# Layer 1's projections of a two-layer backbone: the recurrence's input first, its pieces paced wider

## The chip, the core and the metric

The kernel runs on one core of one Trainium2 chip. The metric is the device time of one execution in microseconds (us); the median of several runs counts.

## The reference, cut to what matters

Two layers work on 1024 latent tokens and 256 context tokens of width 1024. The change lies at the start of layer 1's token mixer:

```python
def mixer_cd(hl, hc, w_in, ...):
    xb_l, gt_l, cq_l, ckv_l, kr_l = split(hl @ w_in)
    xb_c, gt_c, cq_c, ckv_c, kr_c = split(hc @ w_in)
    hf_l, hf_c = rglru_direction(xb_l, xb_c, ..., False)
    hb_l, hb_c = rglru_direction(xb_l, xb_c, ..., True)
    c_l = ((hf_l + hb_l) * jax.nn.gelu(gt_l.astype(jnp.float32))).astype(hl.dtype)
    qn_l, qr_l = mla_q(cq_l, q_norm, w_uq)
    kn_l, v_l = mla_kv(ckv_l, kv_norm, w_ukv)
    kn_c, v_c = mla_kv(ckv_c, kv_norm, w_ukv)
    d_l = mla_latent(qn_l, apply_rope(qr_l, cos, sin), qr_l, kn_l, apply_rope(kr_l, cos, sin), v_l,
                     kn_c, kr_c, v_c)
```

The input, already normed and modulated, is projected to five parts: the recurrence's input xb (512 columns), its gate gt (512), the queries cq (384), keys and values ckv (256) and the rotary key kr (32). The recurrence (a gated linear recurrence, forward and backward, that starts in the context) needs xb of latent and context tokens. cq and ckv are each divided by the root of their mean square per token before the attention uses them.

## The kernel before, in words

Everything is kept transposed: features on the 128 partitions, tokens along the free axis, in three groups of tokens g = 0, 1 (512 latent tokens each) and 2 (256 context tokens). A float32 product is made of three fp32r matmuls per 128 rows of the contraction (`gemm`, L310 on: high weight by high and low input, low weight by high input, L315 to L317), so one projection of one weight tile of 128 columns by one group is 8 x 3 = 24 matmuls into one PSUM bank. There are four such banks (`bank`). A weight tile is loaded by a DMA on SP's queue (`load_w`, L290) into one of two buffers, split on ScalarE (L295) and on GpSimd or VectorE by turns (L298) into one of two pairs of buffers.

`proj1` (L1095 on) makes layer 1's projections by a string of letters, `PROJ1`: x (`p_xb`, four weight tiles for groups 0 and 1, then the same four for group 2), c (`p_cq`, three tiles, groups 0 and 1), k (`p_kv`, two tiles, three groups), g (`p_gt`, four tiles, groups 0 and 1) and r (`p_kr`, one tile, three groups). Results of x, c and k are copied out of PSUM by VectorE (L1157, L1110) and stored to HBM; those of g go through Gelu on ScalarE (L1203); those of r are rotated by VectorE (L1184 to L1188).

Beside the projections run flows: generators that yield a number of units and go on when that many have been pumped. Each projection pumps 8 x max(256, tokens) / 800 units into every flow:

```python
        pump(n * max(256, ps.shape[1]) / 800.0)
```

A projection of 512 tokens is worth 5.12 units, one of 256 tokens 2.56. `drain` runs a flow to its end at once. The instructions of each engine come into an order that a planner makes from this order of writing, and it lets an instruction that is ready go ahead of one that isn't. The flows here:

- "norm": the end of layer 0 for the context (`update`, `postnorm`, `prenorm`, L480 on). It waits YU = 14 units for a reload of x, 3 for the first root, 4 x 1.5 in the post-norm, 18 x 0.6 ahead of the second root, 6 for it and 4 x 2 in the pre-norm, whose tiles hh and hl (L496 to L503) are the input of group 2. Who asks for group 2 earlier forces the flow on (`Lazy`).
- "lru": the recurrence (`lru`, L995 on), in four blocks of 128 features. A block: load xb, 3 units; taps of the convolution on VectorE (L1013, L1017), eight instructions; wait `LY[0]` (10 for block 0); four gates of three matmuls (L1035, two passes each) and three sigmoids (L1036), `LY[1]` after each; tanh; the next block's taps, if its input is there; `LY[2]`; exponentials and squares on ScalarE, two products on VectorE (L1051); `LY[3]`; square roots (L1054); `LY[4]`; for each of two directions a product (L1057) and two scans (L1059, L1061) on VectorE, `LY[5]` after each; a sum on GpSimd (L1063) and the store to hsd (L1064). Block i may start when the context part of x's tile i is written. The gates' buffers r and i are two each: a block's gates need the scans of the block before to be done.
- "nrm": the norms of c and k (`normed`, `fin`, L1100 on). After `KY[0]` units, for each group: sums over partitions by small matmuls (L436), a chain of eleven small VectorE instructions for the inverse root (L440 to L445) and the diagonal tile dg (L452); `YR` = 6 units later a matmul that spreads the root (L457), a reload, the scaling (L1123) and a store; then `KY[1]` units. The squares are summed in a tile with the tag "sq", of which there are three, and dg is one of them too; therefore `normed` drains "nrm" before it begins.
- "mul": the recurrence's output times the gate (L1138 to L1142), from 30 units after both are there.

Ahead of g's last tile (`VW` = 3) the attention's value weights are loaded and split into two pages of a pool of 24. After the last projection "lru" and "nrm" are drained. Then the attention (`mla`) opens its pool where the recurrence's tiles lay: its first tile, va, is filled by ten memsets on GpSimd (L1258), which wait until the memory is free; keys and values are reloaded (L1220) and split (L321, L322), and TensorE starts with the values (L1274 to L1276) and keys.

Of the kernel before, what the change touches and what calls it, by code (L numbers as in the profile page):

```python
# [34 lines left out]
SQB = 3  # L35
# [19 lines left out]
PVD = 4  # L55
PB1 = 6
VW = 3
KY = 3.0, 8.0
CW0 = 2
YU = 14.0  # L60
PACE = 2.3
N0 = "SG"
QE0 = "VGG"
LY = (2.0, 1.0, 1.0, 2.0, 1.0, 1.0)
GY = 30.0, 4.0
DH = "s"
DL = "s"
QE00 = "GVV"
KE = "VV"
LY0 = 10.0  # L70
PROJ1 = "cxkgr"
ORD0 = "BABABABABB"

PO1 = (), ("n+++++nn",)
# [24 lines left out]
def tile_backbone(ctx: ExitStack, tc: tile.TileContext, a: dict, out: bass.AP):  # L99
# [23 lines left out]
    def nm(s):  # L123
        uid[0] += 1
        return f"{s}{uid[0]}"
# [78 lines left out]
    def tmp(n=512, dt=F32):  # L204
        return tp.tile([128, 512], dt, tag="t512", name=nm("t"), bufs=4)[:, 0:n]
# [254 lines left out]
    class Sq:  # L460

        def __init__(self, n, plan="n+++++++", eng="G"):
            self.n, self.acc, self.plan, self.eng, self.i = n, [], plan, V if eng == "V" else G, 0

        def add(self, src):
            new = self.i == 0 or self.plan[self.i] == "n"
            self.i += 1
            t = tp.tile([128, 512], F32, tag="sq", name=nm("sq"), bufs=SQB)[:, 0:self.n] if self.i == 1 else tmp(self.n)
            S.activation(t, src, AF.Square)  # L469
            if new:  # L470
                self.acc.append(t)
            else:
                self.eng.tensor_add(self.acc[-1], t, self.acc[-1])  # L473

    def rstd(sq, d, res, yr=YR):
        dg = rstd_a(sq.acc, sq.n, d)
        yield yr
        res.append(rstd_b(dg, sq.n))
# [616 lines left out]
    def proj1(hs, w, pa, tab, KR, wv):  # L1095

        def x5(s, n):
            return pa.tile([128, 1289], F32, tag=s, name=nm(s), bufs=n)

        def normed(nt, gs, c0, dst, key, d):  # L1100
            drain("nrm")
            sq = [Sq(TOK[g]) for g in gs]
            for i in range(nt):
                wt = wcol(w, c0 + i * 128)
                for g in gs:
                    n = TOK[g]
                    ps = bank()[:, 0:n]
                    gemm(ps, wt, *hs[g])
                    t = tmp(n)
                    V.tensor_copy(t, ps)  # L1110
                    nc.sync.dma_start(dst[:, i, OFF[g]:OFF[g] + n], t)
                    sq[g].add(t)

            def fin():
                yield KY[0]
                for g in gs:
                    n = TOK[g]
                    r = []
                    yield from rstd(sq[g], d, r)
                    for i in range(nt):  # L1120
                        t = tmp(n)
                        nc.sync.dma_start(t, dst[:, i, OFF[g]:OFF[g] + n])
                        V.scalar_tensor_tensor(t, t, cols(key, i), r[0], ALU.mult, ALU.mult)  # L1123
                        nc.sync.dma_start(dst[:, i, OFF[g]:OFF[g] + n], t)
                    yield KY[1]
            spawn(fin(), "nrm")

        def gated(i, key):
            ready.setdefault(i, set()).add(key)
            if len(ready[i]) < 2:  # L1130
                return

            def mul():
                yield GY[0]
                for g in range(2):
                    sl = slice(OFF[g], OFF[g] + 512)
                    t, t2 = tmp(), tmp()
                    nc.sync.dma_start(t, cld[:, i, sl])  # L1138
                    nc.sync.dma_start(t2, hsd[:, i, sl])
                    yield GY[1]  # L1140
                    V.tensor_mul(t, t, t2)
                    nc.sync.dma_start(cld[:, i, sl], t)  # L1142
            spawn(mul(), "mul")

        ready, todo = {}, set()
        GW, sp, tiny = lru_setup(pa)
        spawn(lru(todo, x5, GW, sp, tiny, gated), "lru")
        def p_xb():
            for gs in ((0, 1), (2,)):
                for i in range(4):  # L1150
                    wt = wcol(w, i * 128)
                    for g in gs:
                        n = TOK[g]
                        ps = bank()[:, 0:n]
                        gemm(ps, wt, *hs[g])
                        t = tmp(n)
                        V.tensor_copy(t, ps)  # L1157
                        nc.sync.dma_start(xbd[:, i, OFF[g]:OFF[g] + n], t)
                    if gs == (2,):
                        todo.add(i)  # L1160

        def p_cq():
            normed(3, (0, 1), 1024, cqd, "qn", 384)

        def p_kv():
            normed(2, (0, 1, 2), 1408, kvd, "kvn", 256)

        def p_kr():

            wkr = load_w(w[:, 1664:1696].rearrange("(k p) m -> p k m", p=128), 8, 32)  # L1170
            stg = wrp.tile([128, 8, 128], F32, tag="wr", name=nm("stg"))
            G.memset(stg[:, :, 0:64], 0.0)
            gcopy(stg[:, :, 96:128], wkr[:, :, 0:32])
            rot_w(stg[:, :, 64:96], wkr[:, :, 0:32])
            wt = split_w(stg)
            for g in range(3):
                n = TOK[g]
                ps = bank()[:, 0:n]
                gemm(ps, wt, *hs[g])
                sl = slice(OFF[g], OFF[g] + n)  # L1180
                if g < 2:
                    t = tmp(n)
                    t2 = tmp(n)
                    V.tensor_mul(t[64:96], ps[64:96], tab[64:96, sl])  # L1184
                    V.tensor_mul(t2[64:96], ps[96:128], tab[96:128, sl])
                    V.tensor_add(KR[64:96, sl], t[64:96], t2[64:96])
                else:
                    V.tensor_copy(KR[96:128, sl], ps[96:128])  # L1188

        def p_gt():  # L1190
            for i in range(4):
                if i == VW:
                    raw = wrp.tile([128, 8, 128], F32, tag="wr", name=nm("wr"))
                    src = a["mla_w_ukv"][0].rearrange("(k p) (h t m) -> t p k h m", p=128, t=2, m=64)
                    for k in range(2):
                        nc.sync.dma_start(raw[:, 4 * k:4 * k + 4].rearrange("p a (h m) -> p (a h) m", m=64), src[1, :, k])
                    wv.extend(split_w(raw, pages=True))
                wt = wcol(w, 512 + i * 128)
                for g in range(2):
                    ps = bank()  # L1200
                    gemm(ps, wt, *hs[g])
                    t = tmp()
                    S.activation(t, ps, AF.Gelu_apprx_tanh)  # L1203
                    DQ[DL].dma_start(cld[:, i, OFF[g]:OFF[g] + 512], t)
                gated(i, "g")

        for p in PROJ1:
            {"x": p_xb, "c": p_cq, "k": p_kv, "r": p_kr, "g": p_gt}[p]()
        drain("lru")
        drain("nrm")  # L1210
# [616 lines left out]
```

## Time and profile before

| what | us |
|---|---|
| median of three runs | 3098.53 |
| lowest, highest run | 3087.58, 3100.79 |
| the profiled execution: its own time | 3100.69 |
| its span, first to last instruction | 3098.9 |
| TensorE matmul busy | 2942.0 (95%) |
| VectorE busy | 1747.0 (56%) |
| ScalarE busy | 1093.4 (35%) |
| GpSimd busy | 990.6 (32%) |
| mean granted TensorE clock | 0.974 |

Matmuls are pipelined and their ends are modelled, so the time from one matmul's start to the next one's tells more than the length of one. The granted clock is a share of full speed: 1.0 is 2.4 GHz, half of it 1.2 GHz. "Idle before" in a row is the time that the engine stood still ahead of the instruction, and the name behind the arrow is what ended it.

### The profile page before, as it was taken

The page shows a single profiled execution, that of the slowest core. Times are in us where ns is not written, and L with a number is a line of the kernel's source. Part 1 is how long each engine was busy: PE and PEld are TensorE (multiplying, and loading weights), DVE is VectorE, ACT ScalarE, POOL GpSimd, SP SyncE. Part 2 cuts the span into 40 slices and gives each one's busy share as a digit, 9 for nine tenths or more (in the row PEclk, how much of TensorE's full clock was granted, in tenths as well). Part 3 has the DMA queues.
Part 4 walks back from the last instruction along what each step waited for, and adds up shares of the span by engine and source line. Part 5 has one row for each costly group of instructions (what it writes and reads, how often), then busy time and mean ns, then how long its engine had stood idle before and what let it go on. Part 6 is the DMA issues. An engine that isn't in the chain of part 4 may idle for free. (4 is left out here: it accounts for less than half of the span.)

```text
span 3098.9 us, 37481 instructions
## 1 busy us (share of the span) xinstructions
PE 2942.0 (95%) x14441; PEld 2356.5 (76%) x14441; DVE 1747.0 (56%) x2631; ACT 1093.4 (35%) x1631; POOL 990.6 (32%) x730
## 2 busy tenths in 40 slices
PE   7997899899999999999999889999998999999998
PEld 4886777778888888889997556666686888888886
DVE  4799883665654455568545986667355132232234
ACT  4213884532221112145433763333344222111213
POOL 4676546821110011055432341110253222112223
PEclk8998999999999999999999899999998999999999
DMA  8343113434442344269744230010152121111212
GB/s 295 119 129 100 37 34 111 147 101 129 139 136 82 116 144 145 88 195 281 246 155 152 94 111 26 31 38 28 57 160 89 48 62 55 34 41 55 61 41 109
DMA packets 330768, 327.04 MB, mean 106 GB/s; under 512 B 27121, under 2 KB 280734, under 8 KB 330590
## 3 DMA queue, kind: packets, MB, share of 16 engines
q1 hardware_dynamic: 326784, 321.74, 32.3%
q10 hardware_dynamic: 3806, 2.91, 0.3%
q8 instruction: 113, 1.85, 0.2%
q14 instruction: 65, 0.53, 0.1%
HBM read 255.36 MB, written 69.21 MB: 105 GB/s over the span
## 5 line engine op out<-in xcount | busy, mean ns | idle before, releaser
L298 POOL TENSOR_TENSOR wl<-wr,wh 128x1024 fp32r<-128x1024 f32 x154 | 379.9, 2468 | 1314.2 <-ACT wh L295 1283.1
L295 ACT CAST wh<-wr 128x1024 fp32r<-128x1024 f32 x248 | 259.9, 1049 | 1072.3 <-PE big L316 682.3
L315 PE MATMUL big<-hh,wh 128*128 128x512 f32 x1376 | 541.2, 394 | 4.9 <-DVE ga L1485 2.6
L316 PE MATMUL big<-hl,wh 128*128 128x512 f32 x1376 | 538.6, 392 | 3.1 <-POOL hl L503 3.1
L317 PE MATMUL big<-hh,wl 128*128 128x512 f32 x1376 | 538.8, 392 | 0.6 <-DVE wl L298 0.6
L315 PE MATMUL mm<-hh,wh 128*128 128x256 f32 (+1 forms) x1000 | 346.0, 346 | 9.6 <-DVE i L1031 9.5
L316 PE MATMUL mm<-hl,wh 128*128 128x256 f32 (+1 forms) x1000 | 339.0, 339 | 4.0 <-POOL hl L503 2.0
L317 PE MATMUL mm<-hh,wl 128*128 128x256 f32 (+1 forms) x1000 | 338.0, 338 | 3.2 <-POOL wl L298 2.5
L315 PEld LDWEIGHTS big<-hh,wh 128*128 128x128 f32 x1376 | 260.7, 190 | 61.9 <-ACT hh L498 3.4
L316 PEld LDWEIGHTS big<-hl,wh 128*128 128x128 f32 x1376 | 260.4, 189 | 58.9 <-POOL hl L503 4.3
L317 PEld LDWEIGHTS big<-hh,wl 128*128 128x128 f32 x1376 | 260.5, 189 | 55.6 <-DVE wl L298 1.0
L1553 PE MATMUL mm<-zh,wh 128*128 128x512 f32 x704 | 276.6, 393 | 1.2 <-ACT xt L1656 0.7
L1554 PE MATMUL mm<-zl,wh 128*128 128x512 f32 x704 | 275.0, 391 | 0.3 <-DVE zl L322 0.3
L1555 PE MATMUL mm<-zh,wl 128*128 128x512 f32 x704 | 275.2, 391 | 0.0
L1560 DVE TENSOR_TENSOR acc<-acc,mm 128x512 f32<-128x512 f32 x224 | 150.5, 684 | 178.7 <-PE mm L1555 178.5
L473 POOL TENSOR_TENSOR sq<-t,sq 128x512 f32<-128x512 f32 (+1 forms) x153 | 194.8, 1276 | 170.2 <-ACT t L469 152.0
L1485 DVE SCALAR_TENSOR_TENSOR ga<-big,C,ga 128x1023 f32<-128x1023 f32 x86 | 110.2, 1281 | 235.1 <-ACT ga L1498 233.8
L315 PEld LDWEIGHTS mm<-hh,wh 128*128 128x128 f32 x1000 | 192.3, 192 | 35.7 <-DVE i L1031 9.9
L316 PEld LDWEIGHTS mm<-hl,wh 128*128 128x128 f32 x1000 | 191.9, 192 | 29.4 <-POOL hl L503 5.0
L317 PEld LDWEIGHTS mm<-hh,wl 128*128 128x128 f32 x1000 | 191.6, 192 | 24.3 <-POOL wl L298 3.3
L398 DVE SCALAR_TENSOR_TENSOR wa<-wm,sc,wa 128x256 f32<-128x256 f32 x280 | 148.9, 556 | 90.4 <-DMA wm<-in_w_mod_dram 87.6
L298 DVE TENSOR_TENSOR wl<-wr,wh 128x1024 fp32r<-128x1024 f32 x94 | 131.5, 1399 | 111.6 <-ACT wh L295 108.6
(350 smaller groups left out, 5278.5 us busy)
## 6 DMA issues: line engine op xcount, KB each, us to landing
wr<-in_ffn_w_up_dram SPq DMA_DIRECT2D x132, 512.0 KB, 4.3
wm<-in_w_mod_dram SPq DMA_DIRECT2D x224, 128.0 KB, 2.2
wr<-in_ffn_w_down_dram SPq DMA_DIRECT2D x44, 512.0 KB, 3.5
wm<-in_w_mod_dram SPq DMA_DIRECT2D x40, 512.0 KB, 6.5
xd<-x SPq DMA_DIRECT2D x38, 512.0 KB, 4.1
x<-xd SPq DMA_DIRECT2D x38, 512.0 KB, 6.6
wr<-in_ab_w_out_dram SPq DMA_DIRECT2D x24, 512.0 KB, 7.2
wdd<-wh SPq DMA_DIRECT2D x22, 512.0 KB, 2.6
```

The costliest lines, as they stand in the source:

```text
L295: S.copy(hi[:, 0:nk, 0:m], raw[:, 0:nk, 0:m])
L298: (G if e[wn[0] % len(e)] == "G" else V).tensor_sub(lo[:, 0:nk, 0:m], raw[:, 0:nk, 0:m], f32(hi[:, 0:nk, 0:m]))
L315: T.matmul(ps, wh, xh[k], start=i == 0, stop=False)
L316: T.matmul(ps, wh, xl[k], start=False, stop=False)
L317: T.matmul(ps, wl, xh[k], start=False, stop=i == n - 1)
L398: V.scalar_tensor_tensor(acc[:, v], raw, sc[:, k, v:v + 1], acc[:, v], ALU.mult, ALU.add)
L473: self.eng.tensor_add(self.acc[-1], t, self.acc[-1])
L1485: V.scalar_tensor_tensor(dst[:, lo:hi], src[:, lo + d - o:hi + d - o], k, dst[:, lo:hi], ALU.mult, ALU.add)
L1553: T.matmul(ps, wh, zh, start=j == j0, stop=False)
L1554: T.matmul(ps, wh, zl, start=False, stop=False)
L1555: T.matmul(ps, wl, zh, start=False, stop=j == j1 - 1)
L1560: V.tensor_add(ys[g][c], ys[g][c], ps)
```

## The change

The order of the projections becomes x, c, k, g, r. The sums of squares of k, the only call with three groups, lie in two pages of the pool, so that `normed` need not drain "nrm"; the drain comes ahead of the value weights in `p_gt`. A root is spread `KY[2]` = 16 units after its chain starts, and 4 units lie between two groups. The recurrence's waits `LY` become 8, 1, 3, 4, 3, 2.

```diff
-KY = 3.0, 8.0
+KY = 3.0, 4.0, 16.0
...
-LY = (2.0, 1.0, 1.0, 2.0, 1.0, 1.0)
+LY = (8.0, 1.0, 3.0, 4.0, 3.0, 2.0)
...
-PROJ1 = "cxkgr"
+PROJ1 = "xckgr"
...
-            t = tp.tile([128, 512], F32, tag="sq", name=nm("sq"), bufs=SQB)[:, 0:self.n] if self.i == 1 else tmp(self.n)
+            if self.i > 1:
+                t = tmp(self.n)
+            else:
+                t = tp.tile([128, 512], F32, tag="sq", name=nm("sq"), bufs=SQB)[:, 0:self.n] if self.t0 is None else self.t0
...
         def normed(nt, gs, c0, dst, key, d):
-            drain("nrm")
             sq = [Sq(TOK[g]) for g in gs]
+            if len(gs) > 2:
+                room = [page([128, 2, 512], F32, "sqk") for _ in range(2)]
+                for g in gs:
+                    sq[g].t0 = room[g // 2][:, g % 2, 0:TOK[g]]
...
-                    yield from rstd(sq[g], d, r)
+                    yield from rstd(sq[g], d, r, KY[2])
...
                 if i == VW:
+                    drain("nrm")
```

## Rows read from the trace of the kernel before

**Rows 1.** Windows: stretch, length, busy us (instructions) by engine, granted clock, DMA share, GB/s.

```profile
1700.00:1720.00 20.00, 17.25 (x83) 13.37 (x81) 19.75 (x15) 16.34 (x17) 8.28 (x7) 1.00 0.24 79
1720.00:1740.00 20.00, 13.29 (x52) 9.82 (x53) 19.70 (x19) 11.29 (x18) 9.15 (x6) 0.74 0.25 73
```

**Rows 2.** What TensorE waited for, 1585.5 to 1885 us: total, times, longest.

```profile
PE mm L315 <- DVE i L1031: 9.5, 1, 9.5
PE mm L1274 <- ACT kvh L321: 6.4, 1, 6.4
PE mm L457 <- DVE dg L452: 5.8, 1, 5.8
PE mm L1274 <- DVE kl L1307: 4.8, 1, 4.8
PE mm L1035 <- ACT r L1036: 2.6, 2, 1.4
```

**Rows 3.** Timeline of TensorE: start, us, instruction, in brackets the idle time before.

```profile
1585.49 0.39 PE L315 MATMUL mm<-hh,wh 128*128 128x512 f32 x1
...
1590.93 0.39 PE L315 MATMUL mm<-hh,wh 128*128 128x512 f32 x1
...
1726.71 0.58 PE L315 MATMUL mm<-hh,wh 128*128 128x256 f32 x1 [9.46 <-DVE i L1031]
...
1731.24 1.02 PE L1035 MATMUL mm<-xc,gw 128*128 128x512 f32 x2
...
1756.59 1.42 PE L315 MATMUL mm<-hh,wh 128*128 128x512 f32 x1
...
1764.56 1.02 PE L1035 MATMUL mm<-xc,gw 128*128 128x512 f32 x2
...
1828.64 0.28 PE L317 MATMUL mm<-hh,wl 128*128 128x256 f32 x1
```

**Rows 4.** Timeline of VectorE and ScalarE around the first long wait.

```profile
1721.47 4.56 DVE L1061 TENSOR_TENSOR_SCAN xc<-r,xc,tt 128x1024 f32<-128x1024 f32 x2
1725.98 0.68 DVE L1110 COPY t<-mm 128x512 f32<-128x512 f32 x1
...
1723.89 1.28 ACT L1036 ACT_TABLE_LOAD   x1 [6.08 <-DVE xc L1061]
```

**Rows 5.** Timeline of VectorE: the root chain among other work, and alone.

```profile
1744.24 0.17 DVE L440 TENSOR_SCALAR mm<-mm 128x4 f32<-128x4 f32 x1 [3.36 <-PE mm L436]
...
1754.70 0.68 DVE L452 TENSOR_TENSOR dg<-ident,rst 128x512 f32<-128x512 f32 x1
...
1779.67 0.17 DVE L440 TENSOR_SCALAR mm<-mm 128x4 f32<-128x4 f32 x1 [3.04 <-PE mm L436]
...
1781.89 0.69 DVE L452 TENSOR_TENSOR dg<-ident,rst 128x512 f32<-128x512 f32 x1
```

**Rows 6.** Timeline of VectorE: taps of one direction, first and last of four instructions.

```profile
1770.24 1.62 DVE L1013 TENSOR_SCALAR ca<-xb,C 128x1283 f32<-128x1283 f32 x1
...
1775.08 1.55 DVE L1017 SCALAR_TENSOR_TENSOR xc<-xb,C,ca 128x1283 f32<-128x1283 f32 x1
```

**Rows 7.** Timeline of ScalarE, VectorE, GpSimd: the last block, from its last gate.

```profile
1802.77 1.63 ACT L1036 ACTIVATE i<-mm,C 128x512 f32<-128x512 f32 x3
...
1812.51 2.89 DVE L1051 SCALAR_TENSOR_TENSOR tt<-xc,tt 128x1283 f32<-128x1283 f32 x2
...
1817.87 2.90 DVE L1057 TENSOR_TENSOR tt<-tt,i 128x1283 f32<-128x1283 f32 x2 [1.68 <-ACT tt L1054]
...
1821.87 4.57 DVE L1061 TENSOR_TENSOR_SCAN xc<-r,xc,tt 128x1024 f32<-128x1024 f32 x2
...
1832.19 2.58 POOL L1258 MEMSET va<- 128x256 f32 x10 [2.90 <-DMA hsd<-xc]
```

**Rows 8.** Timeline of ScalarE: the context's pre-norm, last six of eight tiles.

```profile
1641.62 0.51 ACT L498 ACTIVATE hh<-t,MOD 128x256 fp32r<-128x256 f32 x1 [7.34 <-DVE t L496]
...
1645.27 0.41 ACT L502 CAST hh<-t 128x256 fp32r<-128x256 f32 x1
```

More of the change, by code (lines that the diff above doesn't have):

```diff
@@ L462, in __init__ @@
         def __init__(self, n, plan="n+++++++", eng="G"):
-            self.n, self.acc, self.plan, self.eng, self.i = n, [], plan, V if eng == "V" else G, 0
+            self.n, self.acc, self.plan, self.eng, self.i, self.t0 = n, [], plan, V if eng == "V" else G, 0, None
         def add(self, src):
```

## The prediction

> **What bounds the kernel now.** I read the page first: its slices show TensorE near the ceiling almost everywhere, so what can be won is time in which it stands still or runs slow. Then busy time by windows, where layer 1's projections (from 1585.5 us to 1828.9 us) stand out: between 1700 and 1740 us VectorE is busy 39.45 of 40 us, TensorE only 30.54, and the granted clock falls to 0.74 in the second half [rows 1]. Then what TensorE waited for between 1585.5 and 1885 us [rows 2]: two long waits inside the projections, 9.5 us and 5.8 us, and two at the hand-over to the attention, 6.4 us and 4.8 us. Last the timeline of the engines around these.
>
> A projection of 512 tokens is 24 matmuls and takes 5.44 us when nothing disturbs it (1585.49 to 1590.93); one of 256 tokens has half the columns, 2.7 us [rows 3].
>
> The first long wait: TensorE wants a PSUM bank whose copy stands on VectorE behind block 0's scans. The scan issued at 1721.47 lasts 4.56 us for two, the copy comes at 1725.98, and ScalarE's sigmoids of block 1, which hold other banks, also wait 6.08 us for those scans [rows 4]. The second: the root chain of the key-value norm, 2.9 us when alone (1779.67 to 1782.58), took 11.1 us (1744.24 to 1755.38), because pieces of the recurrence stand between its steps; TensorE stood 5.8 us before the matmul that needs it [rows 2, 5]. So in this stretch VectorE is the bound, and only because the recurrence's pieces come too thick.
>
> **The change, part by part.**
>
> Pacing. A projection pumps the flows by 5.12 units (512 tokens) or 2.56 (256). Before, the recurrence's waits add up to 23 units for block 0 and 15 for each other block, 68 in all, and the room from the moment it may start (two context projections before the end of the recurrence's input) to the end is 5.1 + 25.6 (k) + 41.0 (g) + 12.8 (r) = 84.5. After: 31 + 3 x 29 = 118 units, and with c behind x the room is 84.5 + 30.7 = 115.2. VectorE's work for one block is two directions of taps at 6.4 us (1770.24 to 1776.63) [rows 6], 2.89 us for two products, and 8.6 us from the next product to the end of the scans (1817.87 to 1826.44) [rows 7]: 24.3 us a block, 97 in all. It was to go in 72 units (76.8 to 148.5, counting from the first projection), and now in 115. On that count block 0's scans come at 76.8 and block 1's gates, which need their buffers, at 87.0, two projections later; before, the scans and the first gate fell on the same point (105.0). So the first long wait should go: 9.46 us, and the slow matmuls behind it, 4.53 us for 24 instead of 2.7 (1726.71 to 1731.24) [rows 3]: 11.3 us.
>
> Roots later. The root's matmul comes 16 units after the chain starts and not 6: three projections, some 16 us, against a chain that took 11.1 at worst [rows 5]. That takes away 5.8 us and the slow run behind it, 7.97 us for 24 (1756.59 to 1764.56) [rows 3] instead of 5.44: 8.3 us. What is late next there is nothing that TensorE needs. Of the 2.6 us that it waited for gates on ScalarE [rows 2] I count half as gone, 1.3. Together **-20.9 us**.
>
> The input first. Twelve projections with their 12 copies on VectorE, 12 stores and 8 weight loads on SP move ahead of c's six projections, six copies, six squares on ScalarE, four adds on GpSimd, six stores and three loads. None is added; weights are read in the same rhythm of one tile per two projections, and the four context projections, one tile each, stand in a row as before. But x's second half needs the context rows of the layer's input. Their update takes 47.8 units of waits (14 + 3 + 6 + 10.8 + 6 + 8); c and x's first half gave 71.7 before it was asked for, x alone gives 41.0. So six of eight tiles are forced out at once and TensorE waits for them. Before, six tiles took 4.06 us on ScalarE (1641.62 to 1645.68) [rows 8], 0.68 each; eight, with one and a half steps for the first scaling and the last subtraction (my choice), take 6.5 us, less the 2.7 us of projection that runs along: **+3.8 us** (bounds 0 and 6.5).
>
> Sums of squares in pages. No instruction is added; the key-value sums no longer need the three buffers, so the forced end of c's norm ahead of k goes. That cost nothing before: the recurrence's input lay between them.
>
> The forced end moves to the last gate weight (the value weights need those pages). By the pump's count c's norm runs until 128, k's begins then, and at 138.2 only its first root has been started. Three roots are then issued in a row. Covered by nothing, TensorE would wait for the other direction's product and scans (half of 8.6 us) and two chains, 4.3 + 2.9 + 2.9 = 10.1 us; with VectorE as thick as at 1744 us, two chains at 11.1, 22 us. Against that stand two projections of 10.9 us that need none of it, if the plan puts them in between; that queues here leave program order where something isn't ready shows in the 11.1 us of the chain, between whose steps tap and scan pieces stand [rows 5]. I take **+4 us** (bounds 0 and 22), nearer the cover.
>
> New bursts. Between c1 and the end of k VectorE gets block 0's last pieces, two blocks of taps and block 1's, near the 52 us that TensorE needs there. Copies may be late again: **+1.5 us** (0 to 9.5, the old wait).
>
> The hand-over. The recurrence's last block starts its gates at 148.5 units, not 138.2, and its last scan is issued behind the last projection. Before, the time from the end of the last gate on ScalarE (1804.40) to the memset of the value tile, which waits for the recurrence's last store to give its memory free, was 27.8 us [rows 7]. After the change three r projections, 13.6 us, are all that TensorE has behind those gates, so the memset would come some 15 us behind the last of them instead of 3.3 us (1828.92 to 1832.19) [rows 3, 7]: 12 us later. But TensorE waits 6.4 and 4.8 us there anyway [rows 2], and the splits of its inputs can go on meanwhile. **+5 us** (0 to 12).
>
> Sum: -20.9 + 3.8 + 4 + 1.5 + 5 = -6.6 us. On the profiled execution's own 3100.69 us that is 3094.1; it lay 2.2 us above the median, so 3092.
>
> A rule that speaks against the change: the gates, exponentials, roots and Gelus of this stretch need different activation tables, and a load of 1.28 us stands ahead of block 1's gates [rows 4]. The Trainium skill, "ScalarE: Activation LUTs", section "Table sets: the hidden batching unit", says to batch calls by table set. By that rule block 2's three separate groups between Gelus could pay two loads each, six times 1.28 or 7.7 us, and the sum would be +1 instead of -6.6, inside rival A's bounds, if ScalarE were on the path. ScalarE was busy 16.34 and 11.29 of 20 us in the thickest stretch [rows 1], so I don't count it.
>
> **The rivals.** About half a per cent, 15.5 us, is what a measurement of this kernel can tell from no change; the three runs shown lie 13 us apart.
>
> A, the forecast: the two long waits go, the context, the forced roots and the hand-over take back two thirds. -16 to +5 us. For it: each place has its row. Chance 0.52.
>
> B, the takings stay small: the plan fills the gap at the forced roots, and the hand-over's own waits swallow the late tail. Then -20.9 + 3.8 = -17.1 us, or -20.9 with the context hidden: 3078 to 3081. For it: at the hand-over the old path led through r's copies on VectorE, which were late behind block 3's scans and now come before them. Chance 0.27.
>
> C, slower: the three roots run in program order and VectorE is thick there, 22 us, and the tail costs its full 12: -20.9 + 3.8 + 22 + 1.5 + 12 = +18 us, 3117. With the tail at 12 it decides from 19 us of waits before the root matmuls. Against it: 10.9 us of projections at hand. Chance 0.10.
>
> D, VectorE is as full as before: 97 us of recurrence now shares the stretch with c's and k's copies, which are VectorE's, so the 9.5 and 5.8 us waits come again one phase earlier, and only their slow matmuls go: -4.3 + 3.8 + 5 = +4.5 us, 3103. For it: copies stood behind scans [rows 4]. Chance 0.11.
>
> **How the numbers follow.** A is the likeliest: 3092. B lies below, D and C above. From 3076 (B with a few us) to 3106 (D, and A with two of its costs at the bound) no more than 2 in 10 is left out. Faster by over 0.5% (under 3083) is B: 0.27. Slower by over 0.5% (over 3114) is C: 0.10. The rest of A and D: 0.63.
>
> **What would show it.** The waits on L1031's memset and on the first dg should be gone from the list of TensorE's waits, and the clock should stay at 1.00 from 1660 to 1800 us. A wait of some 4 us before the first 256-token projection, released by hh or hl (L498 to L503), shows the context. Waits before L457 just ahead of the last gate projections show the forced roots. The memset of va, released by the store to hsd, should stand some 15 us behind the last projection. I would be wrong if copies at L1110 hold TensorE up again, or if the hand-over's first matmul comes no later than 6.4 us behind the last projection.

## The result, and the profile after

| | before | after |
|---|---|---|
| median of the runs | 3098.23 us (4 runs) | 3128.95 us (4 runs) |
| ratio, 95% interval | | 1.0101 [1.0088, 1.0115] |
| profiled execution / its span | 3100.69 / 3098.9 us | 3127.53 / 3125.7 us |
| projections: first matmul to end of the last | 243.3 us | 261.4 us |
| hand-over: from there to value tile 2 | 25.0 us | 36.3 us |
| from value tile 2 to the end | 1245.1 us | 1242.8 us |

The kernel became 1% slower, 31 us, where 3092 was forecast and 3106 was the upper end. The last three lines come from the two traces: the stretch from 1585 us on, cut at the end of the last projection and at the first matmul of the value projection's tile 2 (the fifth at L1274 before, L1281 after). Some 18 us were lost inside the projections and 11 us behind them; 2 us came back later: 27 us, by which the two profiled executions lie apart (the medians lie 31 us apart). The lines of the changed kernel are 3 to 7 higher than those quoted so far.

What TensorE waited for in the changed kernel, 1585.5 to 1920 us (total, times, longest), answers to [rows 2]:

```profile
PE mm L457 <- DVE dg L452: 19.2, 2, 9.9
PE mm L1283 <- DVE kvl L322: 10.4, 1, 10.4
PE mm L317 <- POOL wk L1289: 7.8, 1, 7.8
PE mm L1038 <- DVE t L1116: 4.6, 1, 4.6
PE mm L1038 <- DVE rst L445: 3.6, 1, 3.6
...
PE mm L316 <- DVE hl L502: 1.5, 1, 1.5
...
PE mm L315 <- ACT hh L501: 1.2, 1, 1.2
```

The waits on the gates' memset and on ScalarE's `r` are gone from the head of the list. In their place stand the spread roots (first line), the hand-over (next two), two new waits of gate matmuls, and the context (last two). The windows of the changed kernel, 20 us each with the columns of [rows 1], show where:

```profile
1700.00:1720.00 20.00, 16.65 (x69) 11.58 (x70) 15.79 (x23) 9.06 (x16) 4.54 (x6) 0.91 0.31 96
1720.00:1740.00 20.00, 20.00 (x107) 16.98 (x106) 15.63 (x15) 14.78 (x14) 6.67 (x4) 1.00 0.40 125
1780.00:1800.00 20.00, 10.70 (x49) 8.09 (x48) 16.54 (x38) 9.16 (x10) 6.50 (x2) 0.79 0.40 131
1800.00:1820.00 20.00, 10.14 (x34) 8.14 (x35) 6.54 (x18) 1.64 (x2) 3.51 (x18) 0.61 0.35 101
```

The stretch that was thick before [rows 1] is loose now: in its second half VectorE is busy 15.6 of 20 us and TensorE all 20. But from 1780 to 1820 us TensorE is busy only 20.8 of 40 us at a granted clock of 0.79 and 0.61, and from 1800 on no engine is busy much over half the time. Something is waiting in a chain there.

**The forced roots.** Timeline of TensorE in the changed kernel, from the forced end of k's norm (start, us, instruction, idle time before):

```profile
1786.62 1.02 PE L457 MATMUL mm<-dg,ones 128*128 128x512 f32 x2
1787.48 0.95 PE L436 MATMUL mm<-ones,sqk 128*128 128x1 f32 x8
1797.73 2.04 PE L457 MATMUL mm<-dg,ones 128*128 128x512 f32 x2 [9.30 <-DVE dg L452]
1799.56 0.85 PE L436 MATMUL mm<-ones,sqk 128*128 128x1 f32 x4
1810.28 1.22 PE L457 MATMUL mm<-dg,ones 128*128 128x256 f32 x2 [9.86 <-DVE dg L452]
1810.94 0.99 PE L315 MATMUL mm<-hh,wh 128*128 128x512 f32 x1
```

Between the second and the last row, 23.5 us, TensorE does nothing but 12 column sums and 4 spreading matmuls. Not one matmul of the last gate weight stands between them: TensorE took everything in the written order. The 24 matmuls behind them run slow, 7.81 us instead of 5.44, at a granted clock of 0.71. VectorE in the same stretch:

```profile
1788.03 4.57 DVE L1064 TENSOR_TENSOR_SCAN xc<-r,xc,tt 128x1024 f32<-128x1024 f32 x2
1792.51 0.72 DVE L1129 SCALAR_TENSOR_TENSOR t<-t,C,mm 128x512 f32<-128x512 f32 x1
1793.15 0.16 DVE L440 TENSOR_SCALAR mm<-mm 128x4 f32<-128x4 f32 x1
...
1795.91 1.67 DVE L452 TENSOR_TENSOR dg<-ident,rst 128x512 f32<-128x512 f32 x1
1799.81 0.75 DVE L1129 SCALAR_TENSOR_TENSOR t<-t,C,mm 128x512 f32<-128x512 f32 x1 [2.23 <-PE mm L457]
1802.04 0.75 DVE L1129 SCALAR_TENSOR_TENSOR t<-t,C,mm 128x512 f32<-128x512 f32 x1 [1.48 <-DMA t<-kvd]
1802.70 0.16 DVE L440 TENSOR_SCALAR mm<-mm 128x2 f32<-128x2 f32 x1
...
1808.66 1.23 DVE L298 TENSOR_TENSOR wl<-stg,wh 128x1024 fp32r<-128x1024 f32 x1 [2.81 <-ACT wh L295]
1809.81 0.42 DVE L452 TENSOR_TENSOR dg<-ident,rst 128x256 f32<-128x256 f32 x1
```

The chain for the second root starts at 1793.15, 5.7 us after its column sums began, because scans and a scaling stand ahead of it. The chain for the third stands behind two scalings of the second root's rows, one of which waits for its reload; and its last step, the diagonal, stands behind a weight split at L298, that of r's weight, which is needed only after the last gate weight. That split waits for ScalarE:

```profile
1807.59 1.04 ACT L295 CAST wh<-stg 128x1024 fp32r<-128x1024 f32 x1 [17.13 <-POOL stg L219]
```

and ScalarE for GpSimd's shuffle of that weight. So a root of 256 tokens was ready at 1806 us but for one 0.42 us instruction, and waited 4 us for a weight of a later projection.

The last gate weight wasn't free of the roots either. ScalarE and GpSimd in the same stretch:

```profile
1788.46 1.99 ACT L295 CAST wh<-wr 128x1024 fp32r<-128x1024 f32 x2 [1.05 <-PE mm L436]
1790.53 4.21 POOL L298 TENSOR_TENSOR wl<-wr,wh 128x1024 fp32r<-128x1024 f32 x1 [17.36 <-ACT wh L295]
```

The first of these two casts is that of the value weights, which needs a page that the second root's column sums have read; the last gate weight's cast stands behind it, and its low half, on GpSimd, ended at 1794.7 us. In two_step_roots below TensorE waits for both halves. So this weight's projections could have covered the waits only from 1790 us on, and fully only from 1795.

**The context.** TensorE in the changed kernel at the first projection of the context rows:

```profile
1632.03 0.51 PE L315 MATMUL mm<-hh,wh 128*128 128x256 f32 x2 [1.19 <-ACT hh L501]
1634.03 0.39 PE L316 MATMUL mm<-hl,wh 128*128 128x256 f32 x1 [1.49 <-DVE hl L502]
```

**The hand-over.** VectorE, GpSimd and TensorE of the changed kernel behind the last projection (1846.6 us), answering to [rows 7]:

```profile
1850.34 4.57 DVE L1064 TENSOR_TENSOR_SCAN xc<-r,xc,tt 128x1024 f32<-128x1024 f32 x2
...
1855.40 4.37 DVE L322 TENSOR_TENSOR kvl<-t,kvh 128x512 fp32r<-128x512 f32 x4
...
1855.08 2.34 POOL L1066 TENSOR_TENSOR xc<-xc,xc 128x1024 f32<-128x1024 f32 x1 [18.37 <-DVE xc L1064]
1860.56 1.57 POOL L1265 MEMSET va<- 128x256 f32 x6 [3.15 <-DMA t<-kvd]
...
1870.43 0.72 POOL L1289 TENSOR_TENSOR wk<-wr,wk 128x256 fp32r<-128x256 f32 x1
...
1858.02 0.79 PE L1283 MATMUL mm<-wh,kvl 128*128 128x512 f32 x1 [10.40 <-DVE kvl L322]
...
1871.20 0.80 PE L317 MATMUL mm<-kvh,wk 128*128 128x512 f32 x1 [7.79 <-POOL wk L1289]
```

The splits of the key-value rows (L322) stand on VectorE behind the last scans; the first of TensorE's two long waits is for them, the second for the weight split on GpSimd, behind the memset and the copies that could start only at 1860.56. That memset comes 14.0 us behind the last projection; the prediction had said 15.

Taken as time over the undisturbed duration of each group of matmuls (5.44 us for 24 of 512 tokens, 2.88 for 256), the projections' excess was 26 us before and 44 after (each line to about 1 us):

| place | before | after |
|---|---|---|
| first long wait with its slow matmuls | 11.3 | 0 |
| root wait in the middle, with its slow matmuls | 9.3 | 1.6 |
| gates held by ScalarE | 3.1 | 0 |
| gates held by a copy (1698 us) or by a chain (1749 us) | 0 | 11.5 |
| the context | 0 | 5.1 |
| forced roots | 0 | 23.5 |
| weights | 2.5 | 2.0 |

### The profile page after: what moved, and what is told of

Same layout as the page of the kernel before. It is cut to its first block, busy times and chain, and to the rows that moved or that the text cites. A ratio compares the mean times of both kernels' runs of the same rounds, so it can differ in the third digit from the quotient of the medians.

```text
span 3125.7 us, 37475 instructions
## 1 busy us (share of the span) xinstructions
PE 2945.8 (94%) x14441; PEld 2358.2 (75%) x14441; DVE 1733.7 (55%) x2631; ACT 1092.7 (35%) x1630; POOL 989.4 (32%) x730
## 5 line engine op out<-in xcount | busy, mean ns | idle before, releaser
L298 POOL TENSOR_TENSOR wl<-wr,wh 128x1024 fp32r<-128x1024 f32 x154 | 381.5, 2478 | 1290.1 <-ACT wh L295 1269.4
L298 DVE TENSOR_TENSOR wl<-wr,wh 128x1024 fp32r<-128x1024 f32 x94 | 132.4, 1409 | 104.7 <-ACT wh L295 101.3
```

The source lines that it names most:

```text
L298: (G if e[wn[0] % len(e)] == "G" else V).tensor_sub(lo[:, 0:nk, 0:m], raw[:, 0:nk, 0:m], f32(hi[:, 0:nk, 0:m]))
```

## The experiments

Thirteen kernels, in the order in which they ran. "Against after" and "against before" say which kernel a diff starts from. Ratios are to the kernel before in the same batch.

**wide_short** (against after): the roots' old rhythm, so that the forced end finds nothing left.

```diff
-KY = 3.0, 4.0, 16.0
+KY = 3.0, 2.0, 6.0
```

> The changed kernel with roots spread 6 units after their chain and 2 units between groups (KY = 3, 2, 6); everything else as changed. By the units, k's third root is then spread at 133, ahead of the drain at 138, so nothing is forced. Theory (the forced roots cost their waits, the late recurrence costs the hand-over): the two waits of 10 us each before L457 ahead of the last gate projections go, with the slow matmuls behind them some 23 us, and the 10.4 and 7.8 us at the hand-over stay: 3128.95 - 23 = 3106 us, still 0.2 to 0.3% above the kernel before. Rival (VectorE has no room in this order, the root chains only wait somewhere else): single waits before L457 come back in the middle of c and k, some 10 to 15 us of them, 3116 to 3121 us.

Measured: 3115.63 us, ratio 1.0048 [1.0032, 1.0063]. Projections 245.8 us, hand-over 36.2. The forced roots are gone and 13 us of the loss with them, but 5.0 us of waits before L457 came back in their old form, with slow matmuls behind them. The time lies beside the rival's band, the waits are half of what the rival said or less. The hand-over didn't move.

**narrow_long** (against after): the old pacing, the long roots.

```diff
-LY = (8.0, 1.0, 3.0, 4.0, 3.0, 2.0)
+LY = (2.0, 1.0, 1.0, 2.0, 1.0, 1.0)
```

> The changed kernel with the recurrence's waits of before (LY = 2, 1, 1, 2, 1, 1); roots still spread 16 units later, so the forced roots stay. Theory: the recurrence then ends at 113 units instead of 161, so the hand-over's waits of 10.4 and 7.8 us shrink to those of the kernel before (6.4 and 4.8 us), -11 us; VectorE is free when the roots are forced, so the two waits of 10 us before L457 shrink to about 5 us each, -10 us; against it the dense pieces give back one wait of up to 10 us in c or k: 3129 - 21 + 8 = 3116 us, between 3106 and 3122. Rival (the hand-over's waits belong to the order x first, not to the late last block): 10 us and more stay at the hand-over, 3126 us or more.

Measured: 3124.54 us, ratio 1.0081 [1.006, 1.0102]. The hand-over fell by 15.2 us to 21.1, but the projections rose by 9.1 to 270.5: of what one place gave, the other took more than half. The time lies between the theory's band and the rival's.

**mid_short** (against after): a pacing in between, the short roots.

```diff
-KY = 3.0, 4.0, 16.0
+KY = 3.0, 2.0, 6.0
...
-LY = (8.0, 1.0, 3.0, 4.0, 3.0, 2.0)
+LY = (4.0, 1.0, 2.0, 3.0, 2.0, 1.0)
```

> The changed kernel with KY = 3, 2, 6 and the recurrence's waits between the two (LY = 4, 1, 2, 3, 2, 1): its last scans are issued at 133 units, a good 28 ahead of the end, and no root is forced. Theory: both costs go, 23 us and 11 us, and the wait for the context (5 us) stays; the pieces are denser than in the changed kernel, which may cost 0 to 8 us: 3129 - 34 + 4 = 3099 us, between 3093 and 3104, at the kernel before or a little faster. Rival (VectorE has no room): dense pieces beside c's and k's copies cost 10 to 20 us, 3105 to 3115 us.

Measured: 3113.04 us, ratio 1.0043 [1.0028, 1.0059]: the rival. Projections 262.3, hand-over 22.4 us.

**mid_short_ctx** (against mid_short): the context's update gets the time that it needs before it is asked for.

```diff
-            yield (YP2 if gi == 2 else YP) * (1 if g < 2 else 0.6)
+            yield (YP2 if gi == 2 else YP) * (1 if g < 2 else 0.2)
```

> The same with the context's wait ahead of its pre-norm 18 x 0.2 units instead of 18 x 0.6, so that its update takes 40.6 units, just under the 41.0 that the recurrence's input for groups 0 and 1 gives. Theory: of the 5 us that TensorE waits for the context's rows ahead of the first 256-token projection 3 to 5 go against the kernel with LY = 4, 1, 2, 3, 2, 1 and KY = 3, 2, 6 alone: 3095 us. Rival (the chain of the norm itself is what it waits for, not the units): no difference, within 2 us.

Measured: 3111.22 us, ratio 1.004 [1.003, 1.005]. In the trace the context's excess fell from 5.5 us in mid_short to 1.7 and the stage by 5.3, so what the rival gave as the reason is not so; but the medians differ by only 1.8 us, which is the rival's number. The runs of the two kernels scatter over 6 and 12 us, so that 1.8 us can't be told from nothing. The context's place is right; what it costs at the end is not shown.

**two_step_roots** (against after): of each of k's roots only the column sums, the chain and the diagonal come ahead of the last gate weight; the spreading matmul follows later.

```diff
+                if len(gs) > 2:
+                    for g in gs:
+                        dgs[g] = rstd_a(sq[g].acc, TOK[g], d)
+                        yield KY[1]
+                    chained.append(key)
                 for g in gs:
...
-                    yield from rstd(sq[g], d, r, KY[2])
+                    if dgs:
+                        yield 4.0
+                        r.append(rstd_b(dgs[g], n))
+                    else:
+                        yield from rstd(sq[g], d, r, KY[2])
...
-                    drain("nrm")
+                    pumping[0] = True
+                    while not chained:
+                        advance(flows["nrm"])
+                    pumping[0] = False
```

> The changed kernel, but only the first half of each of k's three roots (the column sums, the chain on VectorE and the diagonal) is issued or forced ahead of the last gate weight; the matmul that spreads a root follows at least four units later, so each has a projection of its own between. That half is all that has to read the pages. Theory (the forced roots cost 23.5 us because TensorE keeps the written order: the spreading matmul stands ahead of the last two gate projections, and VectorE's chain comes late behind scans and reloads): the waits before L457 ahead of the last gate weight go, 15 to 23 us less in the projections; the time is 3106 to 3114 (ratio 1.003 to 1.005). Rival (VectorE simply has that much work there, and whatever stands behind it waits instead): copies or gates are late by the same amount, 3124 or more.

Measured: 3116.77 us, ratio 1.0056 [1.0043, 1.0069]: 12.2 us less than the changed kernel, between the theory's band and the rival's, nearer the theory. TensorE in this kernel at the same place:

```profile
1782.45 1.39 PE L436 MATMUL mm<-ones,sqk 128*128 128x1 f32 x12
1785.48 0.50 PE L315 MATMUL mm<-hh,wh 128*128 128x512 f32 x1 [1.64 <-ACT wh L295]
...
1788.38 0.80 PE L317 MATMUL mm<-hh,wl 128*128 128x512 f32 x1 [1.71 <-POOL wl L298]
...
1812.88 1.02 PE L457 MATMUL mm<-dg,ones 128*128 128x512 f32 x2
```

All twelve column sums in a row, then projections, and the spreading matmul 27 us later with no wait. That shows that about half of the loss was the place of the spreading matmuls in the written order. The projections fell by 11.6 us, not 15 to 23: the split of the last gate weight is now what TensorE waits for (3.4 us, and matmuls at a granted clock of 0.69 around these waits, some 7 us in all), and the last block's gates take 3 us more.

**roots_only** (against before): the prediction's second term alone.

```diff
-KY = 3.0, 8.0
+KY = 3.0, 4.0
...
-                    yield from rstd(sq[g], d, r)
+                    yield from rstd(sq[g], d, r, 10.0)
```

> The kernel before with its order, its pacing and its sums of squares, and only the spreading matmul of a root put off from 6 to 10 units (the pause behind it cut from 8 to 4, so that nothing is left at the end). Theory (the second long wait of the kernel before is the chain, late by some 4 us behind pieces of the recurrence, and later matmuls cover it): the wait of 5.8 us ahead of L457 and its slow run go, 6 to 9 us, 3090 to 3094 (ratio 0.997 to 0.998). Rival (VectorE has no room there: the reloads' scaling and the copies come later and hold up something else): within 2 us of before, or slower.

Measured: 3098.72 us, ratio 0.9996 [0.9988, 1.0005]. The wait before L457 is gone from the trace (9.3 us with the stretched matmuls behind it), but gate matmuls behind it now wait for ScalarE: 4.2 and 1.6 us instead of 2.6. The projections are 2.4 us shorter, and the runs show nothing: the rival. The interval still allows a gain of up to 4 us.

**wide_fast_tail** (against after): wide pacing for blocks 0 to 2, narrow for the last, short roots, the context at 0.2.

```diff
-KY = 3.0, 4.0, 16.0
+KY = 3.0, 2.0, 6.0
...
-LY = (8.0, 1.0, 3.0, 4.0, 3.0, 2.0)
+LYS = [(8.0, 1.0, 3.0, 4.0, 3.0, 2.0)] * 3 + [(2.0, 1.0, 1.0, 2.0, 1.0, 1.0)]
...
-                    yield LY[1]
+                    yield LYS[i][1]
```

> The input first with the wide pacing for blocks 0 to 2, the old narrow pacing for block 3 alone, the roots in the old rhythm (3, 2, 6 units, so that none is forced), and the context update's pause cut from 0.6 to 0.2. Theory (the projections are short with the wide pacing, 246 us; the hand-over is set by when the last block's last scan is issued, 25 us for unit 148, and this puts it near 145): stage 242 to 246 plus 25, 267 to 271 us, against 268.3 before; time 3095 to 3102. Rival (VectorE has no room: block 3 in a thick row makes copies and roots late again): projections of 255 us or more, 3107 or more.

Measured: 3114.25 us, ratio 1.0052 [1.004, 1.0064]: the rival in time, though the projections are shorter than it said. Projections 250.6 us, hand-over 28.8; the last block's gates now held TensorE up at 1806 us (8.5 us with the stretched matmuls behind).

**narrow_short** (against after): the order alone, with the pages.

```diff
-KY = 3.0, 4.0, 16.0
+KY = 3.0, 2.0, 6.0
...
-LY = (8.0, 1.0, 3.0, 4.0, 3.0, 2.0)
+LY = (2.0, 1.0, 1.0, 2.0, 1.0, 1.0)
```

> The input first, the old narrow pacing for all blocks, the roots in the old rhythm (3, 2, 6 units; none forced): the order alone, with the pages. Theory (pacing trades: a dense recurrence under c's and k's copies holds the projections up, but ends early): projections of 258 to 266 us, hand-over of 21 us, 3105 to 3113. Rival (the order itself costs nothing and the forced roots were all of it): projections of 243 to 250 us, 3090 to 3097.

Measured: 3114.76 us, ratio 1.0053 [1.0038, 1.0067]; projections 264.3, hand-over 20.9 us: both as the theory said, the time 2 us above its band. What TensorE waited for in it, 1580 to 1890 us:

```profile
PE mm L457 <- DVE dg L452: 8.6, 2, 4.4
PE mm L315 <- ACT r L1039: 7.9, 1, 7.9
PE mm L1038 <- ACT r L1039: 7.7, 1, 7.7
PE mm L1281 <- DVE kl L1314: 5.7, 1, 5.7
PE mm L1038 <- DVE i L1034: 4.0, 1, 4.0
```

With the old pacing the new order has the old waits, and more of them, since c's and k's copies and roots now share the stretch with the recurrence.

**gap1** (against before): the prediction's largest term alone. Block 0 starts earlier, and more units lie between its scans and block 1's gates.

```diff
-LY0 = 10.0
+LY0 = 5.0
...
-            yield LY0 if i == 0 else LY[0]
+            yield LY0 if i == 0 else 7.0 if i == 1 else LY[0]
```

> The kernel before with one pacing number changed for one block: block 0 starts its gates 5 units earlier (pause 5 instead of 10) and block 1's gates come 7 units, not 2, behind the issue of block 0's scans; in units everything from block 1's gates on stays where it was. This is the largest term of the prediction, the first long wait (11.3 us), alone. Theory (a wait that is taken from one place comes back at the next one, since VectorE's 97 us of recurrence stand in the same stretch): the first long wait shrinks to 5 us or less, other waits grow, the time is within 4 us of before (ratio 0.9987 to 1.001). Rival (the waits are local, and only pacing makes them): projections of 230 to 234 us instead of 243, the time 3086 to 3089 (ratio 0.996 to 0.997).

Measured: 3095.86 us, ratio 0.9991 [0.9983, 1.0]: the theory; projections 243.7 us, as before. What TensorE waited for in it, 1583.6 to 1880 us:

```profile
PE mm L1035 <- ACT r L1036: 7.5, 2, 4.1
...
PE mm L1035 <- DVE i L1031: 4.7, 1, 4.7
```

The wait on the memset halved, from 9.5 to 4.7 us, and the gates of blocks 2 and 3 wait 7.5 us for ScalarE's sigmoids, which wait for the scans of the block before them: 2.6 us before [rows 2]. The wait moved to the next blocks.

**gap1_roots** (gap1 and roots_only together).

> Both edits in the old order: block 0's gates 5 units earlier and 7 units between its scans and block 1's gates, and the spreading matmul of a root at 10 units instead of 6. Theory (waits come back elsewhere): within 5 us of before. Rival (local waits; with the first one gone the later root pays too): 3082 to 3088, ratio 0.995 to 0.997.

Measured: 3094.85 us, ratio 0.9987 [0.9978, 0.9996]: the theory again. Projections 239.6 us, 3.6 less than before. It is the best kernel of the study, about a tenth of a per cent below the kernel before.

**tail_two_step** (against after): two_step_roots, the last block in the narrow pacing as in wide_fast_tail, the context at 0.2.

> The changed kernel with three edits: k's roots in two halves (only the first forced ahead of the last gate weight), block 3 of the recurrence in the old narrow pacing, the context update's pause 0.2. Theory (forced roots 12, the hand-over up to 11, the context 2 to 5 us are what the change lost, and they are separate places): 3098 to 3106. Rival (VectorE has no room for a dense last block beside the chains and reloads): the projections grow by what the hand-over wins, 3111 or more.

Measured: 3110.49 us, ratio 1.0037 [1.0023, 1.0051], between the two. Projections 244.1 us, as long as before; but the hand-over 32.0 us, with a first wait of 13.2 us for the key-value reload. The waits of gates behind a copy and a chain are still there, 5.6 and 3.6 us.

**gap1_roots_st and tail_two_step_st** (against gap1_roots and tail_two_step): the recurrence's stores on another queue.

```diff
-DH = "s"
+DH = "g"
```

> As the run with both edits in the old order (3094.9), and the recurrence's stores of its output issued from GpSimd's queue, behind the addition that it does itself, instead of from SP's. In the old order the reloads of the key-value rows stand on SP behind the last such store, which waits for the last scans, and TensorE starts the attention's first matmul 5.7 us behind the last projection. Theory (SP's queue holds the reloads): they go out as soon as SP is free, the first wait falls to 3 us or less, the time is 1 to 4 us lower than without, 3090 to 3094. Rival (the value tile's memory, which the last store gives free, sets the hand-over by itself): the first matmul comes earlier, value tile 2 doesn't, the time is within 2 us of 3095.

> As the changed kernel with the three edits (3110.5), and the recurrence's stores issued from GpSimd's queue. There the first matmul of the attention came 13.4 us behind the last projection, released by the key-value reload. Theory (the reloads stand on SP behind the last store): the first wait falls to 5 us or less, the hand-over from 32 to 25 us or less, the time is 3102 to 3107. Rival (the last store's own end, behind the last scans, sets the hand-over, whatever the queue): value tile 2 within 3 us of where it was, 3108 to 3112.

Measured: 3098.09 us, ratio 0.9997 [0.9988, 1.0006], and 3114.34 us, ratio 1.0046 [1.0031, 1.0061]: no gain in either, value tile 2 within 0.4 us of where it was, counted from the last projection. The theory is out; it is the rival, except that the first matmul came no earlier either and that both times lie 1 to 2 us above the rival's. SP and VectorE in tail_two_step_st show why (SPq is SP's queue of DMA issues):

```profile
1827.04 0.44 SPq L1157 DMA_DIRECT2D t<-hsd  x1
1838.34 0.32 SPq L1140 DMA_DIRECT2D t<-kvd  x1
...
1830.69 4.57 DVE L1064 TENSOR_TENSOR_SCAN xc<-r,xc,tt 128x1024 f32<-128x1024 f32 x2
...
1836.73 1.58 DVE L1159 TENSOR_TENSOR t<-t,t 128x512 f32<-128x512 f32 x1
```

With the last block's store off SP, the key-value rows' third reload still goes out only at 1838.3 us, right when the gated product at L1159 ends, which stands on VectorE behind the last scans. The queue wasn't the cause. Two pairs of runs point at the end of the scans on VectorE: wide_fast_tail against wide_short and tail_two_step against two_step_roots, which differ in the last block's pacing and the context's pause, end their scans 4.7 and 9.8 us earlier against the last projection, and their hand-over is 7.4 and 6.9 us shorter. Over all runs the hand-over goes with that end, taken against the end of the last projection:

| kernel | last scan ends | hand-over | projections | sum |
|---|---|---|---|---|
| narrow_long | -55.1 us | 21.1 us | 270.5 us | 291.6 us |
| narrow_short | -43.1 | 20.9 | 264.3 | 285.2 |
| mid_short | -23.0 | 22.4 | 262.3 | 284.7 |
| mid_short_ctx | -23.0 | 22.5 | 256.9 | 279.4 |
| gap1_roots | -3.2 | 25.3 | 239.6 | 264.9 |
| gap1_roots_st | -3.2 | 25.1 | 239.2 | 264.3 |
| roots_only | -3.2 | 25.3 | 240.9 | 266.2 |
| gap1 | -2.8 | 24.7 | 243.7 | 268.4 |
| before | -2.3 | 25.0 | 243.3 | 268.3 |
| tail_two_step | +1.4 | 32.0 | 244.1 | 276.1 |
| tail_two_step_st | +1.4 | 32.4 | 247.0 | 279.3 |
| wide_fast_tail | +3.7 | 28.8 | 250.6 | 279.4 |
| after | +8.3 | 36.3 | 261.4 | 297.7 |
| wide_short | +8.4 | 36.2 | 245.8 | 282.1 |
| two_step_roots | +11.2 | 38.9 | 249.8 | 288.7 |

Up to some 3 us ahead of the last projection the scans cost the hand-over some 4 us at most; from there to the last three lines each later us costs about one, though the two tail_two_step kernels lie 3 to 4 us above that and wide_fast_tail 2 below. And among the kernels with the input first and short roots, the earlier the scans end, the longer the projections are. No kernel with the input first has a sum below that of before.

## Why the prediction was wrong

It was wrong in sign and size; its rival C was the way that it went, and C too was short, by 12 us: about what the new waits inside the projections cost beyond its 1.5.

Both signs by which the prediction would know itself wrong came. A copy held TensorE up again, gate matmuls this time (L1038 behind L1116, which was L1110 before, 4.6 us); and the hand-over's first matmul came 0.3 us behind the last projection (1846.9 against 1846.6), though the third then waited 10.4 us. The granted clock, said to stay at 1.00 from 1660 to 1800 us, was 0.95 there. The table loads that it left out of its sum did not grow: 18 of 1.28 us in the projections, 19 before.

**The three forced roots: +4 us taken, 23.5 measured.** This is the step that failed most. The prediction set two projections of 10.9 us against the waits, "if the plan puts them in between", and took as support that queues leave program order: pieces of the recurrence stood between the chain's steps [rows 5]. Those rows are VectorE's. On TensorE the order here stayed the written one, so nothing covered the waits. Nor did the two projections need none of it: their weight's cast stood behind one that waits for the column sums. And the freedom on VectorE made things worse: r's weight split, written later, went ahead of the third diagonal. two_step_roots shows the cause from the other side: with the spreading matmuls written behind the projections the waits before L457 vanish and 12.2 us come back, half of the loss; the late weight keeps some 7 us of the rest. The upper bound of 22 us was about right partly by luck: program order, which rival C named with a chance of a tenth, was half of its reason; the other half, VectorE as thick as before, was not there (16.5 and 6.5 us busy of 20 in the two windows).

**Pacing and later roots: -20.9 us taken.** The waits named did go, with 23.7 us by the table above. (The prediction took 2.7 us for a projection of 256 tokens; undisturbed it takes 2.88, which changes its sum by 0.2 us.) What failed is "what is late next there is nothing that TensorE needs", and the +1.5 us for new bursts, whose bound was 9.5: 11.5 us of new waits came on gates behind a copy and a chain, and 1.6 on a root, so 10.6 us net. The old order shows the same: roots_only takes 9.3 us of waits away and wins nothing that the runs show, gap1 halves the first long wait and lengthens those of the next two blocks. The prediction read each wait as a loss of its own. They were the places at which TensorE and VectorE, tied to each other by four blocks of gates and scans, came together again; with one loosened, the next one holds. For the old order the two runs show this; for the changed kernel it is read from the table. What it argued for rival D, that VectorE's recurrence now shares the stretch with c's and k's copies, is what narrow_short shows.

**The hand-over: +5 us taken, 11.3 measured, bound 12.** The mechanism was right (the last block ends behind the last projection), the size was at its bound: the old waits of 6.4 and 4.8 us were not there to be used, since the same late scans hold up the splits of the key-value rows on VectorE, and TensorE's new waits are 10.4 and 7.8 us. The prediction had let those splits go on meanwhile. The memset of the value tile came 27.0 us behind the end of the last gate (1833.6 to 1860.6), against 27.8 before [rows 7], as it said.

**The context: +3.8 us taken, 5.1 measured**, within its bounds and at the place named. Whether the shorter pause wins at the end what the trace shows, 5.3 us, the runs leave open (1.8 us in the medians).

The sum with the measured terms is -10.6 + 5.1 + 23.5 = +18 us in the projections and +11.3 behind them, less 2.3 later: +27.0, against +26.8 between the two spans.

**What stays open.** tail_two_step takes out the forced roots, the context and part of the hand-over and is still 13 us above before; its projections are as long as before, since the new waits of gates take what the pacing gave, and its hand-over is 32 us though its scans end 3.7 us later than those of before, and why that small lateness costs 7 us there is not shown (tail_two_step_st has the same 32 us). Whether an x-first order can win at all was not settled: none of the ten kernels with that order did.

## What to carry to other kernels

A forced end is priced at its place in the queue of each engine: ask of every instruction that it issues what stands behind it on that engine, and assume nothing slips past it unless a row of that very engine shows it. Where waits of two engines follow one another through several blocks, removing one is worth what a run with only that edit shows, not its length in the list of waits. And when a producer is made to end later, look for what else of the next stage stands on the same engine behind it.

## What the runs showed of the hardware that was not expected

The same two scans took 4.57 us or 6.63 us. VectorE and GpSimd in gap1, blocks 0 and 1:

```profile
1716.96 4.57 DVE L1061 TENSOR_TENSOR_SCAN xc<-r,xc,tt 128x1024 f32<-128x1024 f32 x2
...
1753.29 6.63 DVE L1061 TENSOR_TENSOR_SCAN xc<-r,xc,tt 128x1024 f32<-128x1024 f32 x2
...
1752.67 2.86 POOL L298 TENSOR_TENSOR wl<-wr,wh 128x1024 fp32r<-128x1024 f32 x1 [13.39 <-ACT wh L295]
```

One scan of 1024 takes 2.32 us alone and 4.38 us where a weight split on GpSimd is running when it starts (1752.67 to 1755.53 here); the extra 2.06 us is nearly the 2.24 us that the two share. In the changed kernel a split that began after the scan cost the scan nothing (2.32 us with 2.06 us of overlap) and took 4.21 us itself. The kernel before has two such longer scans too, 4.46 us at 1757.3 and 4.37 us at 1793.7. The Trainium skill, "Trainium Architecture — The Big Picture", section "What this means for kernel authors", says that VectorE and GpSimd share a port pair by an exclusive lock and not by splitting the bandwidth; these numbers agree. So a weight split that the planner puts on GpSimd, off the critical path by its own engine, can lengthen the scans that everything else waits for. Here ScalarE's next sigmoids wait for the longer scan, and TensorE's gates wait 4.1 us for them:

```profile
1757.76 1.28 ACT L1036 ACT_TABLE_LOAD   x1 [3.47 <-DVE xc L1061]
```

How much of that wait the 2.06 us are, no run shows.
